# A constant of the first pool widened from 4 to 64 bytes, so that the tiles behind it start at multiples of 128

## The chip, the cores and the metric

The kernel runs on one core of a Trainium2 chip. Its time is that of the device for one execution, in microseconds; a kernel's time is the median of several runs. The profile comes from one profiled execution of the same program.

## The reference

The reference computes a two-layer encoder on x (512 tokens x 1024) and a memory of 256 tokens, in float32. Per layer:

```python
h = hybrid_mixer(x, ...)              # three branches read x @ w_in (width 5632)
x = layer_norm(ALPHA * x + h, ...)
h = memory_cross_attention(x, mem, ...)  # 4 heads of 128, 256 memory tokens
x = layer_norm(ALPHA * x + h, ...)
h = conv_ffn(x, w_up, conv_k, conv_b, w_down)   # 1024 -> 2 x 2816 -> 1024
x = layer_norm(ALPHA * x + h, ...)
```

The mixer has a windowed attention (branch A), a dense attention with normed queries and keys (B) and a gated token mixing in chunks of 128 (C). Each branch is projected to 1024, multiplied by the sigmoid of its gate, summed, and projected once more. Nearly all of the arithmetic is matrix products with weights that are read once per layer.

## The kernel before

Each product is done as three TensorE matmuls on float32r: every operand is split into a high part and the rest, and `mm3` (L137 to L140) adds high x high, high x low and low x high into one PSUM tile. So each of L138, L139 and L140 issues one third of the large matmuls; each matmul has its own weight load of 128 x 128, and moves 512 or 256 columns.

The tokens lie in four tiles of 128. `xT` (L90) holds the transposed, split activations, [128, 4 token tiles, high/low, 8 k-tiles, 128]. It is in `cpool`, the first SBUF pool, together with the rope tables, the mask, the two identities `ident` and `ident_r`, the parameters `pp`, `hbias` and, last, `mhalf` (L100), which holds the constant -0.5. GpSimd raises variances to that power in `rstd_of` (L197), through a broadcast of the one column. A memset fills it once at the start.

The pools follow one another in SBUF in the order in which they are opened: `cpool`, `wpool` (two raw weight buffers, six split ones called `w`), `big` (six buffers of 16 KB that hold in turn vc, qs, Q, the branches brA, brB and brC, the softmax ring, mh and ml, memT, mkv, qT, oT, x and g), `kv_p`, `sp` and `small`. Sizes are rounded up to 32 bytes. As built before, xT starts at byte 1152 of each partition (9 x 128), ident at 41600 (325 x 128), mhalf at 44608; it has 4 bytes and takes up 32. The first raw buffer is at 44640 (348 x 128 + 96), the first w at 52832 (412 x 128 + 96), the first buffer of big at 101984 (796 x 128 + 96). All buffers of wpool, big, kv_p and sp are multiples of 512 bytes, so all of them start 96 bytes past a multiple of 128.

Which operands meet in a matmul, the moving one first and the weights second, as the profile names them:

- v, u, q and kv projections (`proj_tm`, L202): w and xT, 512 columns, for kv 256
- gates, wq and up-projection (`proj_fm`, L209): xT and w, 512 columns in four pieces of 128, for half steps 256 in two pieces
- branch projections: brA, brB or brC and w; mixer output: w and mh or ml; memory keys: memT and w (256 columns); output of the cross-attention: w and oT; down-projection: w and g
- attention: Kt and Q, PTa or PTb and V, mkv and qT, PTx and mkv
- transposes: ident or ident_r moves, the tile that is transposed is the weights

A planner (`Weights`) loads the weight chunks in the order of the steps on SyncE's queue. ScalarE makes the high part (`split_hi`, L127), VectorE the rest (`split_lo`, L132). A buffer is filled anew when the last step that reads its old chunk has been issued. The steps themselves are listed by hand at the end of `layer`: projections, attention with the gates and branch projections set between its pieces, mixer output, cross-attention, up-projection in 22 pairs of chunks, down-projection in two halves.

Of the kernel before, what the change touches and what calls it, by code (L numbers as in the profile page):

```python
# [10 lines left out]
F32 = mybir.dt.float32  # L11
# [5 lines left out]
P = 128  # L17
# [56 lines left out]
def encoder_kernel(ctx: ExitStack, tc: tile.TileContext, x_in, xt_in, mem_in, w_in, pp_in, ln_in, cln_in, ws_in, co_in, out):  # L74
# [3 lines left out]
    cpool = ctx.enter_context(tc.tile_pool(name="cpool", bufs=1))  # L78
# [18 lines left out]
    ident_r = cpool.tile([P, P], F32R, name="ident_r")  # L97
    pp = cpool.tile([P, PP_N], F32, name="pp")
    hbias = cpool.tile([P, 24], F32, name="hbias")
    mhalf = cpool.tile([P, 1], F32, name="mhalf")  # L100

    def acc_tile(n=512):
        return ps_acc.tile([P, 512], F32, tag="acc", name="acc")
# [35 lines left out]
        nc.tensor.matmul(ps, lhsT=lh, rhs=rl, start=False, stop=False)  # L139
        nc.tensor.matmul(ps, lhsT=ll, rhs=rh, start=False, stop=last)  # L140

# [1 line left out]
    class Weights:  # L143
        def __init__(self):
            self.order, self.pos, self.last = [], {}, []
# [47 lines left out]
    def pump():  # L193
        W.pump(cur[0])

# [1 line left out]
    def rstd_of(var, n, name):  # L197
        r = sm(n, name)
        nc.gpsimd.tensor_tensor(out=r, in0=var, in1=mhalf.to_broadcast([P, n]), op=ALU.pow)  # L199
        return r  # L200
# [62 lines left out]
        return tiles  # L263

    def rope_rot(t1, t2, src, cos, sin, nh, w):
        # rotate-half within blocks of 2*w, on nh heads of 64
        nb = 64 // (2 * w)
        s4 = src.rearrange("p h (b s d) -> p h b s d", b=nb, s=2)
        o4 = t2.rearrange("p h (b s d) -> p h b s d", b=nb, s=2)
        n4 = sin.rearrange("p (b s d) -> p b s d", b=nb, s=2)  # L270
        nc.vector.tensor_tensor(out=t1, in0=src, in1=cos[:, None, :].to_broadcast([P, nh, 64]), op=ALU.mult)
        for s in range(2):
            if nb == 1:
                nc.vector.tensor_tensor(out=o4[:, :, 0, s, :], in0=s4[:, :, 0, 1 - s, :],
                                        in1=n4[:, 0, s, :][:, None, :].to_broadcast([P, nh, w]), op=ALU.mult)
            else:
                nc.vector.tensor_tensor(out=o4[:, :, :, s, :], in0=s4[:, :, :, 1 - s, :],
                                        in1=n4[:, :, s, :][:, None, :, :].to_broadcast([P, nh, nb, w]), op=ALU.mult)
# [6 lines left out]
    def layer(l):  # L285
        K = lambda kind, c: (l, kind, c)
        R = {}
        last_layer = l == NLAYER - 1

# [1 line left out]
        def params():  # L291
            dma = nc.sync if l == 0 else nc.scalar
            dma.dma_start(out=pp, in_=pp_in[l])
            act(hbias, pp[:, PP_GATE:PP_GATE + 24], AF.Copy, scale=0.5)
            cl = kv_p.tile([P, 2, 512], F32, tag="k", name="cln")
            dma.dma_start(out=cl[:, 0, :], in_=cln_in[l, 0].partition_broadcast(P))
            dma.dma_start(out=cl[:, 1, :], in_=cln_in[l, 1].partition_broadcast(P))
            R["cln"] = cl
            wr = p_tile(name="wsraw")
            dma.dma_start(out=wr, in_=ws_in[l])  # L300
            ws = kv_p.tile([P, 2, 4, P], F32R, tag="v", name="ws", bufs=2)
            wr3 = wr.rearrange("p (g i) -> p g i", g=4)
            split_hi(ws[:, 0], wr3)
            split_lo(ws[:, 1], wr3, ws[:, 0])
            R["ws"] = ws
            R["vc"] = big_tile([P, 2, NT, 512], F32R, "vc")
            R["u"] = big_tile([P, NT, 512], F32, "u")
# [9 lines left out]
                nc.gpsimd.tensor_tensor(out=btab[:, i], in0=b4[:, i % 2],  # L317
                                        in1=g[:, None, :].to_broadcast([P, NT, 64]), op=ALU.mult)

# [1 line left out]
        def v_step(t):  # L321
            def fn():
                ps = acc_tile()
                proj_tm(ps, [K("v", c) for c in range(4)], 2, 512, t)
                pump()
                g = p_tile(name="gv")
                act(g, ps, AF.Gelu)
                st, mv = sm(6, "bn6"), sm(2, "mv")
                nc.vector.bn_stats(out=st, in_=g)
                nc.vector.bn_aggr(out=mv, in_=st)  # L330
                ve = sm(1, "ve")
                nc.vector.tensor_scalar_add(ve, mv[:, 1:2], LN_EPS)
                rs = rstd_of(ve, 1, "rs")
                nc.vector.scalar_tensor_tensor(out=g, in0=g, scalar=mv[:, 0:1], in1=R["cln"][:, 0, :],
                                               op0=ALU.subtract, op1=ALU.mult)
                nc.vector.scalar_tensor_tensor(out=g, in0=g, scalar=rs, in1=R["cln"][:, 1, :],
                                               op0=ALU.mult, op1=ALU.add)
                vc = R["vc"]
                split_hi(vc[:, 0, t, :], g)
                split_lo(vc[:, 1, t, :], g, vc[:, 0, t, :])  # L340
            return Step(fn, [K("v", c) for c in range(4)])
# [29 lines left out]
                pump()  # L371
            return Step(fn)

# [1 line left out]
        def q_step(nm, t):  # L375
            chunks = [K(nm + "q", c) for c in range(4)]

            def fn():
                if t == 0:
                    R["qs"] = big_tile([P, NT, 8, 128], F32R, "qs")  # L380
                ps = acc_tile()
                proj_tm(ps, chunks, 2, 512, t)
                pump()
                s3 = ps.rearrange("p (h d) -> p h d", h=8)
                t1 = p_tile((P, 8, 64), name="rt1")
                t2 = p_tile((P, 8, 64), name="rt2")
                if nm == "a":
                    rope_rot(t1, t2, s3, rope[:, 0, t, :], rope[:, 1, t, :], 8, 32)
                    nc.gpsimd.tensor_tensor(out=t1, in0=t1, in1=t2, op=ALU.add)
                else:  # L390
                    rs = rms(s3, p_tile((P, 8, 64), name="rtn"), 8)
                    rope_rot(t1, t2, s3, btab[:, 0, t, :], btab[:, 1, t, :], 8, 16)
                    nc.gpsimd.tensor_tensor(out=t1, in0=t1, in1=t2, op=ALU.add)
                    nc.vector.tensor_tensor(out=t1, in0=t1, in1=rs, op=ALU.mult)
                qs = R["qs"]
                split_hi(qs[:, t, :, 0:64], t1, scale=0.125)
                split_lo(qs[:, t, :, 64:128], t1, qs[:, t, :, 0:64], scale=0.125)
            return Step(fn, chunks)
# [65 lines left out]
                pump()  # L464
            return Step(fn)

# [1 line left out]
        def a_keys(q):  # L468
            return max(0, q - 1), min(NT - 1, q + 1)

# [82 lines left out]
                evac_pv("A", h, ps)  # L553
            return Step(fn, urgent=True)

# [1 line left out]
        def bS_step(u):  # L557
            def fn():
                h, pr = u // 2, u % 2
# [48 lines left out]
                    evac_pv("B", h, R.pop("pv"))  # L608
            return Step(fn, urgent=True)

# [1 line left out]
        def ring():  # L612
            if "ring" not in R:
                R["ring"] = big_tile([P, 8, 512], F32, "ring")
            return R["ring"]
# [58 lines left out]
                f.append(br_step(n, m, stage))  # L674
            return f

# [1 line left out]
        def mix_step(half, t):  # L678
            chunks = [K("mix", half * 4 + c) for c in range(4)]

# [12 lines left out]
                    ln_finish(t, *R["ln"])  # L693
            return Step(fn, chunks)

# [1 line left out]
        def memT_step():  # L697
            def fn():
                R["memT"] = big_tile([P, 2, KD, NMEM], F32R, "memT")
# [138 lines left out]
                ln_finish(t, *R["ln"])  # L838
            return Step(fn, chunks)

# [1 line left out]
        def g_slot(j):  # L842
            if j % 4 == 0 and j < 20:
                R["g", j // 4] = big_tile([P, 4, 2, S], F32R, "g")
# [95 lines left out]
                        nc.sync.dma_start(out=out[t * P:(t + 1) * P, sl], in_=X[0][:, t, sl])  # L940
            return Step(fn, [K("down", 11 + c) for c in cs])

# [1 line left out]
        def st(s):  # L944
            steps.append(s)

# [139 lines left out]
    for l in range(NLAYER):  # L1086
        layer(l)
# [37 lines left out]
            W.pump(i)  # L1125


# [1 line left out]
def _pack_weights(d):  # L1129
    out = np.empty((NLAYER * NCH, P, 1024), np.float32)  # L1130

    def tm(w, c0, n, nk):
        # (K, n) columns c0.. cut in chunks of nk k-tiles: [p, k, n]
        kt = w.shape[0] // P
        a = w[:, c0:c0 + n].reshape(kt // nk, nk, P, n).transpose(0, 2, 1, 3)
        return a.reshape(kt // nk, P, nk * n)

    def fm(w):
        # (K, M) as [m, p, k, 128]
        kt, mt = w.shape[0] // P, w.shape[1] // P  # L1140
        return w.reshape(kt, P, mt, P).transpose(2, 1, 0, 3).reshape(mt, P, kt * P)

    for l in range(NLAYER):
        def put(kind, a):
            i = l * NCH + CHUNK_ID[kind, 0]
            out[i:i + a.shape[0]] = a

        w = d["w_in"][l]
        put("aq", tm(w, 0, 512, 2))
        put("akv", tm(w, 512, 256, 4))  # L1150
        put("bq", tm(w, 768, 512, 2))
        put("bkv", tm(w, 1280, 256, 4))
        put("u", tm(w, 1536, 512, 2))
        put("v", tm(w, 2048, 512, 2))
        put("gate", fm(w[:, 2560:]))
        put("br", np.concatenate([fm(d["w_branch"][l, n]).reshape(4, 2, P, 512).transpose(0, 2, 1, 3).reshape(4, P, 1024)
                                  for n in range(3)]))
        w = d["w_mix_out"][l]
        put("mix", np.concatenate([tm(w, 0, 512, 2), tm(w, 512, 512, 2)]))
        put("wq", fm(d["x_wq"][l]))  # L1160
        w = d["x_wkv"][l]
        put("mk", fm(w[:, :512]))
        put("mv", tm(w, 512, 512, 2))
        w = d["x_wo"][l]
        put("wo", np.concatenate([tm(w, 0, 512, 2), tm(w, 512, 512, 2)]))
        put("up", fm(d["f_w_up"][l]))
        w = d["f_w_down"][l]
        put("down", np.concatenate([tm(w, 0, 512, 2), tm(w, 512, 512, 2)]))
    return out
# [65 lines left out]
```

## Time and profile before

| | |
|---|---|
| time, median of 3 runs | 1843.59 us (1843.54 to 1844.64) |
| span of the profiled execution | 1842.8 us |
| TensorE busy | 1811.5 us, 98% of the span, 9064 matmuls |
| VectorE busy | 1065.9 us, 58% |
| ScalarE busy | 756.0 us, 41% |
| GpSimd busy | 316.4 us, 17% |
| mean granted TensorE clock | 0.994 |
| moved by DMA | 176.60 MB, mean 96 GB/s |

The profile gives the span of the profiled execution, from its first to its last instruction; it has no time of its own beside it, and the median of the runs is 0.8 us above the span. A matmul's duration in a row runs from its start to the end of its result, and overlaps with the next ones; how far apart matmuls follow one another is read from their starts in the timeline, or from the count of matmuls in a window. PEld are the weight loads, which also overlap with matmuls.

### The profile page before, as it was taken

Reading aid. Unit: us, or ns where it says so; the run is one execution under the profiler, and the core shown is the slowest. Engines: PE = TensorE matmul, PEld = TensorE weight load, DVE = VectorE, ACT = ScalarE, POOL = GpSimd, SP = SyncE. Lnnn points to the kernel's source line nnn. Section 1 sums busy time; section 2 is a strip of 40 time slices with the busy share of each in tenths; the row PEclk is TensorE's granted clock in tenths of the full one; section 3 lists DMA queues with packets and bytes.
Section 4 is the critical chain, followed back from the end, with each engine's and each line's share of the span. In section 5 each row is a group of like instructions: output and inputs, shape, how many; then the busy total and the mean of one; then the engine's idle time right before and its main releaser. Section 6 shows DMA issues by size and latency. Waiting matters only on the chain.

```text
span 1842.8 us, 23541 instructions
## 1 busy us (share of the span) xinstructions
PE 1811.5 (98%) x9064; PEld 1516.5 (82%) x9064; DVE 1065.9 (58%) x1728; ACT 756.0 (41%) x1274; POOL 316.4 (17%) x320
## 2 busy tenths in 40 slices
PE   8999999999999999999999999999999999999998
PEld 6888888878978888888888888888789788888886
DVE  5566856557675555533466568565575755555334
ACT  4346635532534443331133565455325244444210
POOL 1112422220131111100011124331201311111000
PEclk9999999999999999999999999999999999999999
DMA  6221221232413222232233212212333222222321
GB/s 221 88 78 65 81 92 58 71 132 95 150 69 103 92 92 92 99 119 92 92 131 105 79 70 83 79 58 81 129 109 130 81 92 92 92 102 92 103 103 46
DMA packets 51233, 176.60 MB, mean 96 GB/s; under 512 B 5681, under 2 KB 6193, under 8 KB 50865
## 3 DMA queue, kind: packets, MB, share of 16 engines
q1 hardware_dynamic: 44784, 158.86, 24.8%
q10 hardware_dynamic: 6336, 16.23, 2.7%
q8 instruction: 72, 1.18, 0.3%
q14 instruction: 41, 0.33, 0.1%
HBM read 170.87 MB, written 4.19 MB: 95 GB/s over the span
## 4 chain that ended last, share of the span: by engine, by line
PE 97%; DVE 1%; ACT 1%; DMA 0%; issue 0%; DVEq 0%; SPq 0%
PE acc L138 26%; PE acc L139 26%; PE acc L140 26%; PE s L567 2%; PE pv L604 1%; PE t L590 1%; PE s L138 1%; PE s L140 1%; PE s L139 1%; PE t L140 1%; PE t L138 1%; PE t L139 1%; PE pv L139 1%; PE pv L549 1%; PE s L483 1%; PE pv L138 1%
## 5 line engine op out<-in xcount | busy, mean ns | idle before, releaser
L132 DVE TENSOR_TENSOR w<-raw,w 128x1024 fp32r<-128x1024 f32 x284 | 354.8, 1250 | 454.0 <-ACT w L127 452.9
L127 ACT ACTIVATE w<-raw 128x1024 fp32r<-128x1024 f32 x292 | 309.4, 1060 | 495.7 <-PE acc L140 276.7
L138 PE MATMUL acc<-xT,w 128*128 128x512 f32 (+1 forms) x1216 | 463.3, 382 | 4.5 <-DVE x L234 4.2
L140 PE MATMUL acc<-xT,w 128*128 128x512 f32 (+1 forms) x1216 | 464.5, 382 | 0.0
L139 PE MATMUL acc<-xT,w 128*128 128x512 f32 (+1 forms) x1216 | 462.6, 381 | 0.0
L138 PEld LDWEIGHTS acc<-xT,w 128*128 128x128 f32 x1216 | 228.4, 188 | 50.1 <-DVE x L234 4.6
L140 PEld LDWEIGHTS acc<-xT,w 128*128 128x128 f32 x1216 | 229.2, 189 | 45.8
L139 PEld LDWEIGHTS acc<-xT,w 128*128 128x128 f32 x1216 | 229.3, 189 | 45.5
L138 PE MATMUL acc<-w,xT 128*128 128x512 f32 (+1 forms) x384 | 138.2, 362 | 7.4 <-ACT w L127 7.2
L139 PE MATMUL acc<-w,xT 128*128 128x512 f32 (+1 forms) x384 | 138.6, 361 | 1.2 <-DVE w L132 1.2
L140 PE MATMUL acc<-w,xT 128*128 128x512 f32 (+1 forms) x384 | 138.4, 360 | 0.0
L870 POOL TENSOR_TENSOR cv<-cv 128x512 f32<-128x512 f32 x44 | 56.8, 1292 | 445.4 <-DVE cv L858 402.2
L199 POOL TENSOR_TENSOR rs<-ve,mhalf 128x1 f32<-128x1 f32 x32 | 30.2, 942 | 422.4 <-DVE ve L244 371.4
L138 PEld LDWEIGHTS acc<-w,xT 128*128 128x128 f32 x384 | 72.8, 189 | 18.9 <-ACT w L127 7.8
L139 PEld LDWEIGHTS acc<-w,xT 128*128 128x128 f32 x384 | 72.6, 189 | 13.5 <-DVE w L132 2.0
L140 PEld LDWEIGHTS acc<-w,xT 128*128 128x128 f32 x384 | 72.7, 189 | 10.8
L502 POOL TENSOR_SCALAR ring<-ring,rsm 128x256 f32<-128x256 f32 (+1 forms) x64 | 43.6, 693 | 186.2 <-DVE rsm L500 108.3
L569 DVE TENSOR_REDUCE nm<-s 128x1 f32<-128x512 f32 x64 | 43.9, 688 | 54.2 <-PE s L567 53.5
L124 ACT ACTIVATE ring<-s,nm 128x512 f32<-128x512 f32 x64 | 44.0, 688 | 69.7 <-PE t L590 45.4
L655 POOL TENSOR_TENSOR mg<-mg,ring 128x512 f32<-128x512 f32 x32 | 47.8, 1498 | 140.4 <-DVE ring L654 112.4
L576 POOL TENSOR_SCALAR ring<-ring,rsm 128x512 f32<-128x512 f32 x64 | 45.7, 727 | 129.7 <-DVE rsm L574 129.7
L124 ACT ACTIVATE cv<-acc,pp 128x512 f32<-128x512 f32 x86 | 65.4, 760 | 1.5 <-PE acc L140 1.5
(237 smaller groups left out, 3302.7 us busy)
## 6 DMA issues: line engine op xcount, KB each, us to landing
raw<-in_w_dram SPq DMA_DIRECT2D x292, 512.0 KB, 3.5
lngb<-in_ln_dram ACTq DMA_DIRECT2D x16, 256.0 KB, 4.3
xraw<-in_xt_dram SPq DMA_DIRECT2D x4, 512.0 KB, 4.7
memr<-in_mem_dram ACTq DMA_DIRECT2D x2, 1024.0 KB, 4.8
x<-in_x_dram ACTq DMA_DIRECT2D x4, 512.0 KB, 7.3
x_keep<-x ACTq DMA_DIRECT2D x4, 512.0 KB, 2.6
x<-x_keep ACTq DMA_DIRECT2D x4, 512.0 KB, 7.5
out_dram<-x SPq DMA_DIRECT2D x8, 256.0 KB, 2.0
```

The source lines that it names most:

```text
L124: return nc.scalar.activation(out, in_, func, **kw)
L127: nc.scalar.activation(out, in_, AF.Copy, scale=scale)
L132: eng.tensor_tensor(out=out, in0=in_, in1=hi.bitcast(F32), op=ALU.subtract)
L138: nc.tensor.matmul(ps, lhsT=lh, rhs=rh, start=first, stop=False)
L139: nc.tensor.matmul(ps, lhsT=lh, rhs=rl, start=False, stop=False)
L140: nc.tensor.matmul(ps, lhsT=ll, rhs=rh, start=False, stop=last)
L502: nc.gpsimd.tensor_scalar(out=pr_t[qi], in0=pr_t[qi], scalar1=rs[:, qi:qi + 1], scalar2=0.0, op0=ALU.mult, op1=ALU.add)
L567: nc.tensor.matmul(ps, lhsT=R["Q"][:, h, q * P:(q + 1) * P], rhs=R["Kt"][:, kv * 2 + hl, :], start=hl == 0, stop=hl == 1)
L569: nc.vector.tensor_reduce(out=nm[:, qi:qi + 1], in_=ps, axis=AX.X, op=ALU.max, negate=True)
L576: nc.gpsimd.tensor_scalar(out=pr_t[qi], in0=pr_t[qi], scalar1=rs[:, qi:qi + 1], scalar2=0.0, op0=ALU.mult, op1=ALU.add)
L655: nc.gpsimd.tensor_tensor(out=mg, in0=mg, in1=tg, op=ALU.add)
L870: nc.gpsimd.tensor_tensor(out=c, in0=ca, in1=c, op=ALU.mult)
```

## The change

mhalf is declared with 16 columns, and the name is bound to its first column. It takes up 64 bytes in place of 32, so every tile of the later pools lies 32 bytes further: raw at 44672 (349 x 128), w at 52864 (413 x 128), big at 102016 (797 x 128). The tiles of cpool stay where they are. The rest of the diff removes comments.

```diff
-    mhalf = cpool.tile([P, 1], F32, name="mhalf")
+    mhalf = cpool.tile([P, 16], F32, name="mhalf")[:, 0:1]
...
-    # ---- weight stream ----
+
```

## The prediction

> **What bounds the kernel now.** I read the page first: its busy times and the chain that ended last.
>
> ```profile
> span 1842.8 us, 23541 instructions
> PE 1811.5 (98%) x9064; PEld 1516.5 (82%) x9064; DVE 1065.9 (58%) x1728; ACT 756.0 (41%) x1274; POOL 316.4 (17%) x320
> PE 97%; DVE 1%; ACT 1%; DMA 0%; issue 0%; DVEq 0%; SPq 0%
> ```
>
> TensorE (PE) has work in 98% of the span and makes up 97% of the chain. The waits of PE come next; the three longest are
>
> ```profile
> PE acc L138 <- ACT w L127: 7.2, 1, 7.2
> PE acc L138 <- DVE x L234: 4.9, 4, 2.1
> PE acc L138 <- ACT brB L127: 4.1, 2, 2.1
> ```
>
> with only some 7 us behind them. So the time is the number of matmuls times the distance from one start to the next, and only a change of that distance moves it. The duration that a row gives for a matmul is no such distance (they overlap), so I read starts in the timeline. This stretch is the most telling one. The name after the arrow is the moving operand, the last one the weights:
>
> ```profile
> 917.33 0.39 PE L140 MATMUL pv<-w,g 128*128 128x512 f32 x1
> ...
> 921.41 0.40 PE L140 MATMUL pv<-w,g 128*128 128x512 f32 x1
> ...
> 922.99 0.40 PE L140 MATMUL acc<-w,xT 128*128 128x512 f32 x1
> ...
> 928.35 0.39 PE L139 MATMUL acc<-w,xT 128*128 128x512 f32 x1
> ```
>
> The first pair spans 18 gaps: 4.08 / 18 = 0.2267 us. The second spans 23: 5.36 / 23 = 0.2330 us. Shape and moving tile are alike; the weights come from g in one and from xT in the other. (The PSUM pool differs too, but matmuls of w and g that write acc go as fast: row four of the windows below.) xT is in the first pool. In the program as built before, xT starts at byte 1152 = 9 x 128, and every tile that TensorE reads from the later pools starts 96 bytes past a multiple of 128 (the first of them at 44640 = 348 x 128 + 96). All offsets inside these tiles are multiples of 512 bytes. So each matmul has either two operands at the same offset (96 and 96, "same") or one at 0 and one at 96 ("mixed", all that use xT). Longer stretches of one kind agree:
>
> ```profile
> 20.00:60.00 40.00, 40.00 (x173) 32.19 (x172) 22.70 (x36) 18.19 (x25) 7.42 (x8) 1.00 0.46 155
> 420.00:450.00 30.00, 30.00 (x134) 24.86 (x133) 18.48 (x28) 4.24 (x4) 1.91 (x2) 1.00 0.34 116
> 600.00:780.00 180.00, 180.00 (x773) 144.60 (x772) 94.09 (x113) 74.48 (x98) 20.66 (x16) 1.00 0.27 94
> 840.00:896.00 56.00, 56.00 (x248) 46.36 (x248) 18.20 (x19) 11.00 (x11) 0.00 (x0) 1.00 0.27 94
> ```
>
> The columns are the window, its length, then busy time and count of PE, weight loads, DVE, ACT and POOL, granted clock, DMA share. Row three is the up-projection (moving xT, weights w, mixed): 180 us over 772 gaps is 0.2332. Row one is the v and u projections (moving w, weights xT, mixed): 40 / 172 = 0.2326, cut at the window's edges. Row two, the mixer output (w and mh, w and ml), and row four, the down-projection (w and g), are same: 30 / 133 = 0.2256 and 56 / 247 = 0.2267. The clock is full in all four. The other engines don't explain it: DVE is busy 57% in row one, 62% in row two, 52% and 33% in three and four.
>
> **The change part by part.** It adds no instruction, wait or transfer. mhalf grows from 4 bytes, which take up 32, to 64; all later tiles move up by 32 bytes, so the 96 becomes 0. xT, rope, the masks and the identities stay. The memset and GpSimd's reads of mhalf go on using one column: nothing. After it every pair of operands has the same offset.
>
> *Mixed matmuls of 512 columns.* The groups by line and form:
>
> ```profile
> L138 PE MATMUL acc<-xT,w 128*128 128x512 f32 x1056 | 418.8, 397 | 0.3
> L138 PE MATMUL acc<-w,xT 128*128 128x512 f32 x256 | 101.8, 400 | 7.4 <-ACT w L127 7.2
> ```
>
> L139 and L140 have as many, so 3 x (1056 + 256) = 3,936. Of these the gates are 2 layers x 24 x 8 x 3 = 1,152; they stand in short bursts between pieces of attention. The other 2,784 run in long stretches: at 0.2333 now, and at the 0.2267 of the down-projection if "same" is what counts, 6.6 ns each or 18.4 us. In the bursts a same pair is not at its best:
>
> ```profile
> 305.62 0.39 PE L140 MATMUL acc<-brA,w 128*128 128x512 f32 x1
> ...
> 307.01 0.39 PE L140 MATMUL acc<-brA,w 128*128 128x512 f32 x1
> ...
> 308.86 0.39 PE L140 MATMUL acc<-xT,w 128*128 128x512 f32 x1
> ...
> 310.26 0.39 PE L140 MATMUL acc<-xT,w 128*128 128x512 f32 x1
> ```
>
> Six gaps each: 0.2317 for brA and w (same), 0.2333 for xT and w (mixed). For the gates the gain lies between 1.6 ns and 6.6 ns; a burst holds both a start and a settled part, so I take 4.1: 1,152 x 4.1 ns = 4.7 us, ends 1.8 and 7.6.
>
> *Mixed matmuls of 256 columns* (kv, and the halves of wq and of the first up chunks):
>
> ```profile
> L138 PE MATMUL acc<-xT,w 128*128 128x256 f32 x160 | 44.8, 288 | 4.2 <-DVE x L234 4.2
> L138 PE MATMUL acc<-w,xT 128*128 128x256 f32 x128 | 36.4, 285 | 0.0
> L138 PE MATMUL pv<-xT,w 128*128 128x256 f32 x32 | 10.6, 331 | 1.0 <-ACT xT L127 1.0
> ...
> 467.05 0.28 PE L139 MATMUL acc<-memT,w 128*128 128x256 f32 x1
> ...
> 467.89 0.28 PE L140 MATMUL acc<-memT,w 128*128 128x256 f32 x1
> ...
> 483.73 0.28 PE L139 MATMUL acc<-xT,w 128*128 128x256 f32 x1
> ...
> 484.20 0.28 PE L140 MATMUL acc<-xT,w 128*128 128x256 f32 x1
> ```
>
> 3 x (160 + 128 + 32) = 960. The same pair memT and w goes at 0.84 / 7 = 0.120, the mixed one at 0.47 / 4 = 0.118. Here "same" is the slower by 2 ns: 1.9 us lost. I take that row; the other end is below.
>
> *Same matmuls.* By the loops some 2,500 of 512 columns: down 1,056, branch projections 576, mixer output 384, wo 192, the rest smaller. They go from 96 and 96 to 0 and 0. No pair at 0 and 0 is in the trace; the nearest row is their own 0.2267, so I take no change. The bounds are under the rivals.
>
> *Transposes.* The identity lies at 0 and what it transposes at 96:
>
> ```profile
> 922.04 0.87 PE t L225 x8
> ```
>
> 0.109 us each. About 860 of them become same. No row shows that; by the 2 ns of the 256-column pairs it is 1.7 us either way, and I take zero.
>
> *What must keep up.* A chunk of up-projection lasts 24 x 0.2333 = 5.60 us and would last 5.44; in it ACT is busy 41% and DVE 52%, and a weight transfer lands in 3.5 us:
>
> ```profile
> raw<-in_w_dram SPq DMA_DIRECT2D x292, 512.0 KB, 3.5
> ```
>
> So the weight stream has cover; without it the next limit of that stage would be DVE's 94 of 180 us. The waits of PE at the stage ends stay, and so does the start. I put 0 to 2 us on their growing and take 0.
>
> Sum: 18.4 + 4.7 - 1.9 = 21.2 us less. The span of the profiled execution is 1842.8, the median of the runs 1843.6, 0.8 us above it; I put the sum on the median: **1822 us**.
>
> The Trainium skill ("TensorE: Matmul & The Clock Gate", Part 2, step 1) says that TensorE has two independent SBUF read ports, and that loading the next weights takes nothing from the running matmul. By that rule the offset of one operand to the other can't matter, the sum is zero and the time stays 1843.6. The two halves of the stretch at 917 to 928 us, 0.2267 and 0.2330 with the same moving tile, don't fit it, if nothing else about xT differs.
>
> **The rivals.**
>
> *No effect:* xT is slow for a reason of its own, where it lies or how it is read, and its offset is not it; nothing changes, 1843.6. (The Trainium skill's rule of the two ports, above, ends here too.) For it: every slow pair has xT, and only xT. Against it: xT is slow both as moving operand in four pieces (row three) and as weights in one piece (row one), by the same amount, so the pieces aren't it; and both operands are only read in either case.
>
> *The offset of 96 itself costs,* beside the mixture: then at 0 and 0 the distance falls further. The floor comes from the start, at half the granted clock:
>
> ```profile
> 9.51 0.63 PE L138 MATMUL acc<-w,xT 128*128 128x512 f32 x1
> ...
> 11.22 0.63 PE L139 MATMUL acc<-w,xT 128*128 128x512 f32 x1
> ```
>
> 1.71 / 4 = 0.4275, so 0.2135 at the full clock. All the way down it is 3,936 x 19.8 ns + 2,500 x 13.2 ns + 960 x 11.3 ns = 122 us, about 1722. Against it: at half the clock the mixed pairs show no excess at all, so the excess may belong to the full rate and not to an offset. The Trainium skill ("TensorE: Matmul & The Clock Gate", "Wait — 56ns, not 53.3ns?") gives columns / 2.4 + 2.5 ns for back-to-back matmuls, for 512 an estimate of 215.8 ns, nearly this floor; the 226.7 of the trace is above it.
>
> *Offset 0 is the slow one* (the other side): in the rows every slow pair has an operand at 0 and no fast one has. If one or both at 0 cost 6.6 ns, the mixed pairs stay and the 2,500 same ones go up: +16.5 us, 1860; if each operand adds its own 6.6, +42, 1886. It decides as soon as the same pairs lose more on their 2,500 than the mixed gain on 3,936, 2,500 lost against 3,936 gained: from 1.6 ns of loss for each ns of gain. For it: the rows alone don't exclude it. Against it: at 256 columns the pairs with an operand at 0 are the faster ones.
>
> **How the numbers follow.** Equal offsets: 0.62; no effect: 0.18; a larger gain: 0.10; slower: 0.10. What this kernel can tell from no change is about 0.2%, 3.7 us. So faster 0.72, same 0.18, slower 0.10. The likeliest case alone reaches from 1804 to 1835: the low end has all 3,936 at 6.6 ns (26.0 us) and the 256 columns at half the 0.2135 (960 x 11.3 ns and 192 of memT x 13.2 ns, 13.4 us); the high end has the gates at their low end, the transposes against it, the waits at 2 us, and the long stretches at two thirds. The range takes in no effect, with the 256 columns alone 2 ns slower (1845.5): **1804 to 1846**; it leaves out the last two cases, 0.20.
>
> **What would show it.** Right: in the up-projection the starts come 0.227 apart, a 180 us window there holds some 795 matmuls in place of 773; the down-projection stays at 248 in 56 us; kv and the halves go to 0.120. Wrong: 773 again (xT's own reason); the down-projection above 0.2267 (offset 0 is slow) or below 0.22 (96 costs); or the distance falls and PE's waits for w grow by as much.

## The result and the profile after

The changed kernel takes 1822.27 us (median of 4 runs, 1821.94 to 1823.06), the one before in the same comparison 1844.05: ratio 0.9881, 95% interval [0.9869, 0.9893]. The forecast was 1822, in a range of 1804 to 1846.

The page of the changed kernel, its busy times and the engines of the chain that ended last:

```profile
span 1820.2 us, 23541 instructions
PE 1789.6 (98%) x9064; PEld 1518.3 (83%) x9064; DVE 1064.8 (58%) x1728; ACT 755.7 (42%) x1274; POOL 317.2 (17%) x320
PE 97%; DVE 1%; ACT 1%; DMA 0%; issue 0%; DVEq 0%; SPq 0%
```

Every engine has as many instructions as before, and TensorE still makes up the chain. The span is 22.6 us shorter, PE's busy time 21.9. PE's waits are as before to within 0.3 us each; it is its own work that got shorter. Its longest waits:

```profile
PE acc L138 <- ACT w L127: 7.1, 1, 7.1
PE acc L138 <- DVE x L234: 4.8, 4, 2.1
PE acc L138 <- ACT brB L127: 4.1, 2, 2.1
```

Three of the four windows of before, read from the changed kernel; the fourth, 420 to 450 us, now takes in eight transposes beside the mixer output, so its count does not compare (window, its length, busy time and count of PE, weight loads, DVE, ACT and POOL, granted clock, DMA share, GB/s):

```profile
20.00:60.00 40.00, 40.00 (x178) 33.13 (x177) 22.73 (x35) 18.75 (x25) 7.29 (x8) 1.00 0.49 154
...
600.00:780.00 180.00, 180.00 (x796) 149.05 (x795) 97.24 (x116) 77.08 (x101) 20.74 (x16) 1.00 0.29 97
840.00:896.00 56.00, 56.00 (x249) 46.37 (x248) 19.57 (x24) 9.56 (x10) 0.72 (x1) 1.00 0.29 94
```

In the up-projection 796 matmuls stand in 180 us where 773 stood: 180 / 795 = 0.2264 us from start to start, before 0.2332. In the v and u projections 178 stand in 40 us, before 173. The down-projection has 249 in 56 us, before 248. The stretch that carried the prediction, where the weights change from g to xT, reads now:

```profile
906.06 0.39 PE L140 MATMUL pv<-w,g 128*128 128x512 f32 x1
...
910.14 0.39 PE L140 MATMUL pv<-w,g 128*128 128x512 f32 x1
...
914.24 0.39 PE L139 MATMUL acc<-w,xT 128*128 128x512 f32 x1
...
916.96 0.39 PE L139 MATMUL acc<-w,xT 128*128 128x512 f32 x1
```

4.08 / 18 = 0.2267 with g, and 2.72 / 12 = 0.2267 with xT: once settled, the two are alike. Just behind the transposes in between it is not yet so: the eleven gaps from 911.70 us to the first of the xT rows shown take 2.54 us, 0.231 each.

### The profile page after: what moved, and what is told of

Read it like the earlier page. It is cut to its first block, busy times and chain, and to the rows that moved or that the text cites. A ratio compares the mean times of both kernels' runs of the same rounds, so it can differ in the third digit from the quotient of the medians.

```text
span 1820.2 us, 23541 instructions
## 1 busy us (share of the span) xinstructions
PE 1789.6 (98%) x9064; PEld 1518.3 (83%) x9064; DVE 1064.8 (58%) x1728; ACT 755.7 (42%) x1274; POOL 317.2 (17%) x320
## 4 chain that ended last, share of the span: by engine, by line
PE 97%; DVE 1%; ACT 1%; DMA 0%; issue 0%; DVEq 0%; SPq 0%
PE acc L138 26%; PE acc L139 26%; PE acc L140 25%; PE s L567 2%; PE pv L604 1%; PE t L590 1%; PE s L139 1%; PE s L138 1%; PE s L140 1%; PE t L139 1%; PE t L138 1%; PE t L140 1%; PE pv L139 1%; PE pv L549 1%; PE s L483 1%; PE pv L138 1%
## 5 line engine op out<-in xcount | busy, mean ns | idle before, releaser
L138 PE MATMUL acc<-xT,w 128*128 128x512 f32 (+1 forms) x1216 | 457.5, 378 | 4.2 <-DVE x L234 4.2
L140 PE MATMUL acc<-xT,w 128*128 128x512 f32 (+1 forms) x1216 | 459.2, 378 | 0.0
L139 PE MATMUL acc<-xT,w 128*128 128x512 f32 (+1 forms) x1216 | 457.4, 377 | 0.0
```

Source lines behind the costliest of these rows:

```text
L138: nc.tensor.matmul(ps, lhsT=lh, rhs=rh, start=first, stop=False)
```

## The experiments

The change does two things at once. It puts all tiles that TensorE reads on multiples of 128, and it makes the start of xT agree with the start of everything else. Theory A: the agreement counts. Theory B, the change's own words: the multiples of 128 count. All layouts below differ from the kernel before only in padding; "n apart" says that the later pools lie n bytes further past xT's start than in the changed kernel, where the distance is a multiple of 256 (before, by the same count modulo 256, n is 224).

**All at 96.** mhalf takes 64 bytes, and 96 bytes stand in front of xT:

```diff
+    front = cpool.tile([P, 24], F32, name="front")
     xT = cpool.tile([P, NT, 2, KD, P], F32R, name="xT")
...
-    mhalf = cpool.tile([P, 1], F32, name="mhalf")
+    mhalf = cpool.tile([P, 16], F32, name="mhalf")[:, 0:1]
```

> All tiles start 96 bytes past a multiple of 128, xT and the identities too (96 bytes in front of xT, mhalf at 64 bytes). If it is the equality of the two operands' offsets that counts: as the changed kernel, 1822 us, some 796 matmuls of the up-projection in 180 us. If it is that tiles start at multiples of 128, as the change says: no better than before, 1844 us or more, 773 matmuls or fewer.

Measured 1822.07 us, ratio 0.9878 [0.9862, 0.9895]. Its up-projection window:

```profile
600.00:780.00 180.00, 180.00 (x796) 149.10 (x795) 97.23 (x116) 77.04 (x101) 20.72 (x16) 1.00 0.29 97
```

No tile that TensorE reads starts at a multiple of 128, and all of the gain is there. Theory B falls on this run.

**128 apart.** The other half of the cross: all tiles at multiples of 128, but not agreeing modulo 256.

```diff
-    mhalf = cpool.tile([P, 1], F32, name="mhalf")
+    mhalf = cpool.tile([P, 48], F32, name="mhalf")[:, 0:1]
```

> All tiles at multiples of 128, but the later pools 128 bytes further than in the changed kernel (mhalf at 192 bytes), so xT starts 128 past a multiple of 512 and they start 256 past. If the period is 128 bytes: 1822 us as the changed kernel. If the period is 256 or 512: 1844 us or another time.

Measured 1842.15 us, ratio 0.9986 [0.9977, 0.9995]:

```profile
600.00:780.00 180.00, 180.00 (x776) 145.97 (x775) 93.97 (x112) 74.78 (x98) 20.65 (x16) 1.00 0.28 94
840.00:896.00 56.00, 56.00 (x248) 46.36 (x247) 17.98 (x19) 11.21 (x11) 0.00 (x0) 1.00 0.27 94
```

This layout does what the change says and has a tenth of its gain. The up-projection is slow (776), the down-projection, whose operands agree, is as fast as ever. So agreement modulo 128 is not enough.

**256 and 512 apart.** mhalf with 80 and with 144 columns, by the same one line. In the first the starts agree modulo 256 and not modulo 512, in the second modulo 512.

> xT starts 128 past a multiple of 512, the later pools 384 past (mhalf at 320 bytes): 256 apart. If the offsets need to be equal modulo 256: 1822 us, 0.2267 us apart in the up-projection. If modulo 512, as the 128 apart leaves open: 1838 to 1845 us, with a pattern of its own.

> The later pools 512 bytes further than in the changed kernel (mhalf at 576 bytes), so all start 128 past a multiple of 512. If equality modulo 512 or less is what counts: 1822 us. If a longer period counts, or if the changed kernel was lucky in where its tiles fell: another time, up to 1844 us.

Measured 1822.03 us (ratio 0.9878 [0.9863, 0.9892]) and 1821.40 us (0.9874 [0.9858, 0.9891]). The window of the first:

```profile
600.00:780.00 180.00, 180.00 (x796) 149.10 (x795) 97.22 (x116) 77.10 (x101) 20.71 (x16) 1.00 0.30 97
```

So the starts have to agree modulo 256. Modulo 512 is not needed: the two runs are as fast as the changed kernel.

**Is it xT, or any two operands?** xT and w as in the changed kernel, 32 bytes between wpool and big:

```diff
-    mhalf = cpool.tile([P, 1], F32, name="mhalf")
+    mhalf = cpool.tile([P, 16], F32, name="mhalf")[:, 0:1]
...
+    gap = ctx.enter_context(tc.tile_pool(name="gap", bufs=1)).tile([P, 8], F32, name="gap")
     big = ctx.enter_context(tc.tile_pool(name="big", bufs=6))
```

> xT and w as in the changed kernel, but 32 bytes between wpool and big, so g, mh, ml, oT, memT and the branches lie 32 past where w lies. If any two operands of unlike offset are slow: the up-projection stays at 0.2267 us, the down-projection, mixer output, wo and branch projections go to 0.233, and the time is 1822 + 2,300 x 6.6 ns, about 1837 us, a little less for the bursts. If xT has something of its own: 1822 us, the down-projection at 0.2267.

Measured 1835.97 us, ratio 0.9951 [0.9936, 0.9966]:

```profile
420.00:450.00 30.00, 30.00 (x131) 24.14 (x130) 18.02 (x27) 4.24 (x4) 1.99 (x2) 1.00 0.33 105
600.00:780.00 180.00, 180.00 (x796) 149.05 (x795) 96.72 (x116) 76.00 (x100) 21.89 (x17) 1.00 0.30 97
840.00:896.00 56.00, 56.00 (x242) 45.08 (x241) 17.01 (x18) 10.60 (x11) 0.00 (x0) 1.00 0.29 94
```

The picture is turned round. The up-projection stays fast (796), and the down-projection, which no layout above had moved, falls to 242: 56 / 241 = 0.2324. So does the mixer output, 131 in 30 us where 134 stood in the kernel before, both windows of mixer output alone. Any two operands show it; xT has nothing of its own.

**The other distances.** mhalf with 24, 32, 40, 56 and 64 columns puts the later pools 32, 64, 96, 160 and 192 bytes past xT.

> xT at 0, the later pools at 32 past a multiple of 128 (mhalf at 96 bytes; the kernel before has them at 96). If equality modulo 128 counts: pairs with xT stay mixed, 1844 us, 0.233 us apart; pairs without xT at 0.2267. If only the 96 was bad: 1822 us. If the distance between the offsets sets the price in steps: between 1822 and 1844 us, or above.

> xT at 0, the later pools at 64 past a multiple of 128 (mhalf at 128 bytes). If equality modulo 128 counts: 1844 us. If the period is 64 bytes or less: 1822 us and 0.2267 us apart in the up-projection.

> The later pools 96 bytes further than xT modulo 256 (mhalf at 160 bytes). With a period of 256: one of the unlike offsets, 0.229 to 0.234 us in the up-projection, 1837 to 1845 us. If some distance is better than equality, one of the three still open (96, 160, 192) would show it: below 1820 us.

> The later pools 160 bytes further than xT modulo 256 (mhalf at 224 bytes). As for 96: 1837 to 1845 us if equality is the best there is; below 1820 us if this distance is better.

> The later pools 192 bytes further than xT modulo 256 (mhalf at 256 bytes). As for 96: 1837 to 1845 us if equality is the best there is; below 1820 us if this distance is better. If the price is the same for plus and minus, as the kernel before (224) and the 32 suggest: near the 1840 us of 64 apart.

| later pools past xT, modulo 256 | time, us | up-projection: matmuls in 180 us | v and u: matmuls in 40 us |
|---|---|---|---|
| 0 (changed) | 1822.27 | 796 | 178 |
| 32 | 1844.28 | 773 | 173 |
| 64 | 1839.92 | 773 | 176 |
| 96 | 1847.86 | 770 | 173 |
| 128 | 1842.15 | 776 | 174 |
| 160 | 1846.86 | 773 | 173 |
| 192 | 1832.58 | 788 | 173 |
| 224 (before) | 1844.05 | 773 | 173 |

No distance beats agreement, so there is no better version among these. 96 and 160 came out slower than their expected 1837 to 1845, and 64 lay between its two forecasts. The expectation that 192 would be like 64 missed too: 1832.58 (ratio 0.9939 [0.9924, 0.9953]) against 1839.92 (0.9975 [0.9966, 0.9984]). The windows of the two, first of 64 apart,

```profile
20.00:60.00 40.00, 40.00 (x176) 32.84 (x175) 23.29 (x36) 18.29 (x25) 7.43 (x8) 1.00 0.48 156
...
600.00:780.00 180.00, 180.00 (x773) 145.05 (x772) 94.71 (x114) 73.74 (x96) 20.70 (x16) 1.00 0.29 94
```

then of 192 apart,

```profile
20.00:60.00 40.00, 40.00 (x173) 32.25 (x172) 23.61 (x36) 19.24 (x25) 7.59 (x8) 1.00 0.51 162
600.00:780.00 180.00, 180.00 (x788) 147.71 (x787) 95.34 (x115) 74.83 (x98) 22.08 (x17) 1.00 0.29 97
```

show why. In v and u w moves and xT is loaded; in the up-projection it is the other way round. Moving operand 64 past the weights: 40 / 175 = 0.2286 (v and u, 64 apart) and 180 / 787 = 0.2287 (up, 192 apart). Moving operand 64 before the weights: 0.2326 and 0.2332. The distance has a sign, and the price goes by moving minus weights. Over the settled matmuls of these two windows in all the traces, the two stages agree at every such distance: 233.3 ns with the moving operand 32 bytes past the weights, 228.9 at 64, 233.3 at 96, 232.4 at 128, 234.3 at 160, 233.3 at 192 and 224, whichever of w and xT moves.

**Is it the weight load's reads?** In the up-projection six of eight k-tiles load and use half of the weight columns:

```diff
-            mm3(ps, w[:, 0, k, :], w[:, 1, k, :], xT[:, ts, 0, k, :], xT[:, ts, 1, k, :], k == 0, k == KD - 1)
+            m = P if k in (0, KD - 1) or key[1] != "up" else P // 2
+            mm3(ps[0:m], w[:, 0, k, 0:m], w[:, 1, k, 0:m], xT[:, ts, 0, k, :], xT[:, ts, 1, k, :], k == 0, k == KD - 1)
```

Once on the layout before, and once on the changed one (mhalf with 16 columns):

> The layout before (mixed), but in the up-projection the six middle k-tiles load and use only 64 of the 128 weight columns; that part of the product is left out for the other half of the channels. If the excess over the 0.2135 floor is the weight load's reads holding up the moving ones: the distance falls from 0.2333 towards 0.224 in those, the time by some 1,440 x 9 ns = 13 us, 1831 us. If it is a cost of each matmul, whatever it loads: 0.2333 and 1844 us stay.

> The changed kernel's layout (equal offsets) with the half-width weight loads: in the up-projection the six middle k-tiles load and use 64 of the 128 weight columns; that part of the product is left out for the other half of the channels. On the layout before, the half loads brought the distance only from 0.2333 to about 0.2315. If the rest of the excess belongs to each matmul and not to what it loads: 0.2267 stays, 796 matmuls in 180 us, 1822 us. If it is the load's reads: 0.220, some 815 matmuls, 1812 us.

One execution each: 1840.27 and 1825.44 us. The window on the layout before:

```profile
600.00:780.00 180.00, 180.00 (x779) 114.98 (x779) 95.37 (x114) 75.19 (x98) 20.60 (x16) 1.00 0.29 94
```

It holds 779 matmuls in place of 773, 180 / 778 = 0.2314 after 0.2332: a fifth of the way to 0.224. On the changed layout neither expectation held. Its matmuls and, below, its loads (PEld):

```profile
600.08 0.40 PE L138 MATMUL acc<-xT,w 128*64 128x512 f32 x1
...
603.99 0.39 PE L140 MATMUL acc<-xT,w 128*64 128x512 f32 x1
604.22 0.39 PE L138 MATMUL acc<-xT,w 128*128 128x512 f32 x1
...
605.36 0.39 PE L140 MATMUL acc<-xT,w 128*128 128x512 f32 x1
```

```profile
603.76 0.13 PEld L140 LDWEIGHTS acc<-xT,w 128*64 128x64 f32 x1
604.00 0.19 PEld L138 LDWEIGHTS acc<-xT,w 128*128 128x128 f32 x1
```

The loads are shorter, 0.13 us for 0.19, and the matmuls with them are slower: 3.91 / 17 = 0.2300, against 1.14 / 5 = 0.228 by these rows for the full ones between (0.2265 over all full ones of the window). So the excess is not simply a price per loaded byte: half the load took 1.8 ns off at unlike starts and added 3.3 at agreeing ones, half of what an unlike start costs. The edit also halves the columns that the matmul itself uses (128*64 in the rows), so it does not separate the load from the matmul. That the excess shifts when the reads of load and matmul meet would fit this, but no run shows it; what happens inside the chip stays open.

## Why the prediction was right

I summed the distances from each matmul's start to the next in both traces, by kind, and set them beside the terms.

- *Long stretches of 512 columns, 2,784 matmuls, forecast -18.4 us:* up-projection and wq -13.1, v, u and q -4.3, together -17.5 (summed before rounding). The windows show the step, from 0.2332 to 0.2264 in the up-projection.
- *Gates in bursts, forecast -4.7 (1.8 to 7.6):* -4.8. The middle between start and settled part was the right size: the mean of the undisturbed distances went from 233.0 to 228.8 ns, 4.2 ns.
- *Mixed pairs of 256 columns, forecast +1.9:* +0.5. The settled distance did go up, from 117.3 to 119.8 ns where xT moves, from 118.4 to 119.6 ns where it is loaded; together some 1.7 us, close to the forecast. The rest lies in stretches with a granted clock of 0.50, which the sum had left out: where xT moves, 47 gaps of 0.21 us stand in them before and 37 after, because one stretch was shorter in the profile after (rows below). Ten such gaps fewer, each some 0.094 us longer than a settled one, are 0.9 of the 1.2 us in question. Whether the shorter stretch has to do with the layout is not shown.
- *Same pairs and transposes, forecast 0:* -0.6 and -0.1. That 0 and 0 would be as 96 and 96 is shown by the run with all at 96.
- *Waits and supply, forecast 0 to 2:* PE's waits are the same to 0.3 us each. The faster up-projection raises DVE to 54% (97 of 180 us), ACT to 43%, with room left.

The sum of the sizes, -22.5, makes up the span's -22.6; the forecast was -21.2.

The stretches at a granted clock of 0.50, each with its window and two rows, first before, then after:

```profile
547.94:554.76 6.82, 5.71 (x25) 5.42 (x26) 6.82 (x12) 1.38 (x2) 0.12 (x1) 0.50 0.25 85
...
550.23 0.41 PE L138 MATMUL pv<-xT,w 128*128 128x256 f32 x1
...
554.49 0.41 PE L140 MATMUL acc<-xT,w 128*128 128x256 f32 x1
```

```profile
545.07:548.48 3.41, 3.03 (x14) 3.04 (x15) 3.41 (x6) 1.06 (x1) 0.00 (x0) 0.50 0.01 4
...
546.04 0.42 PE L138 MATMUL pv<-xT,w 128*128 128x256 f32 x1
...
548.18 0.41 PE L139 MATMUL acc<-xT,w 128*128 128x256 f32 x1
```

The rows are 4.26 / 20 = 0.213 and 2.14 / 10 = 0.214 us apart: at this clock the unlike starts of before and the agreeing ones of after go alike.

One step went further than the trace reached. I put the tiles at "0 or 96" modulo 128 and said that all would be the same when the 96 became 0. The runs show a period of 256: 128 apart would have failed. The change works because xT starts at 1152 and the later pools at 44672, both 128 past a multiple of 256. The trace of before had no pair that agrees modulo 128 and not modulo 256, so it could not tell. That the 32 bytes led to agreement modulo 256 as well was luck.

The rivals: *no effect* falls with the result itself, since xT stayed where it was, and with the run with big 32 further, where other tiles than xT got slow. *96 itself costs* falls with all at 96. *Offset 0 is slow* falls with the down-projection of the changed kernel, 249 in 56 us. Its second price was added up wrongly: if each operand at 0 costs 6.6 ns, the same pairs go from none to two, which gives 3,936 x 6.6 ns + 2,500 x 13.2 ns = 59 us and not 42; the case lay above the range either way.

Against *96 itself costs* stood that mixed pairs show no excess at half the clock. The floor it compares them with is taken from the same rows, and the profile's own figure for the granted clock there is 1.00; half was inferred from the distance. The stretches at 0.50 above show what the argument needed, at 256 columns. At 512, brB and w, which agree, stand 1.28 / 3 = 0.427 apart at 0.50 (1277.02 to 1278.30 us in the changed kernel), as the mixed ones at the start did, 0.4275.

The Trainium skill ("TensorE: Matmul & The Clock Gate", Part 2, step 1) holds that loading the next weights takes nothing from a running matmul, as the two reads have ports of their own. By that no layout here should differ; they differ by up to 1.4% of the kernel (1822 to 1848 us), so the measurement decides. The halved loads, with halved matmuls, moved the distance too, by 3.3 ns up at agreeing starts and by 1.8 ns down at unlike ones, so they are no support for the rule either.

## What to carry to other kernels

When TensorE is busy throughout, read how far apart the starts of its matmuls are, by pair of operands, and not how long each lasts; a few per cent between pairs of one shape can hide in a column of nearly equal durations (397 and 389 ns on average before). Where every matmul has its own weight load, let moving and stationary tiles start at the same place modulo 256 bytes in SBUF (shown here for float32r at 512 columns; for 256 see below); padding of a few dozen bytes can settle it, and any tile added to an early pool can undo it. A cause named in a change is worth a cross of its own: the runs with the named property alone (128 apart) and without it (all at 96) took one or two lines each.

## What was not expected of the hardware

- Where the two operands of a matmul start, relative to each other, changes the distance between matmuls: 0.2267 us at agreement modulo 256 bytes, 0.229 to 0.234 otherwise, for 512 float32r columns with a load of 128 columns each.
- The price depends on the sign: moving 64 bytes past the weights 0.2286, 64 before them 0.2326 to 0.2332.
- A weight load of 64 columns, shorter by 0.06 us, together with a matmul that uses 64, made matmuls of 512 columns slower in the agreeing layout, 0.2300 for 0.2267.
- At a granted clock of 0.50 unlike starts cost nothing: 0.213 us before and 0.214 after, at 256 columns.
- At 256 columns agreement is not the best. In the changed kernel wq's half steps go at 1.20 / 10 = 0.120 us:

```profile
473.02 0.28 PE L139 MATMUL acc<-xT,w 128*128 128x256 f32 x1
...
474.22 0.28 PE L140 MATMUL acc<-xT,w 128*128 128x256 f32 x1
```

With the later pools 64 bytes past xT, 19 gaps of the same step take 2.15 us, 0.113 each:

```profile
470.81 0.28 PE L139 MATMUL acc<-xT,w 128*128 128x256 f32 x1
...
472.96 0.28 PE L140 MATMUL acc<-xT,w 128*128 128x256 f32 x1
```

Giving only the 960 matmuls of 256 columns such a distance would be worth at most 960 x 7 ns = 6.7 us by these rows; over all settled ones that xT moves in the two traces the means are 115.2 and 119.8 ns, so some 4 us is likelier. It was not tried.
